# The down-projection of an MLP by one level of Strassen's scheme, on one Trainium2 core

## The chip, the cores and the metric

The kernel runs on one core of a Trainium2 chip. The core has TensorE (PE, with its weight loads shown as PEld), VectorE (DVE), ScalarE (ACT), GpSimd (POOL) and SyncE (SP), a memory SBUF of 128 partitions, accumulator banks (PSUM) that TensorE writes, and 16 DMA engines. The metric is the device time of one execution in microseconds (us), as the median of several runs.

## The reference

The program is one layer of a hybrid encoder for 1024 prompt tokens and 32 sample tokens, 1056 together. Three mixers (attention, a state space model, RWKV-7) write one merged activation; then

```python
x = layer_norm(ALPHA * x + merged @ prm['w_out'], prm['ln1_g'], prm['ln1_b'])
hidden = jnp.square(jax.nn.relu(x @ prm['w_up']))      # 1024 -> 4096
x = layer_norm(ALPHA * x + hidden @ prm['w_down'], prm['ln2_g'], prm['ln2_b'])   # 4096 -> 1024
```

Everything is float32. The change concerns the last two lines and the end of the first.

## The kernel before

**Products.** A float32 operand is split in a high part (a copy rounded by ScalarE) and a low part (what is left, subtracted by VectorE or GpSimd): `split3`. `mm3` then makes three matmuls per block: high x high, high x low, low x high. Its three lines (63, 65, 67) issue nearly all the matmuls here.

**Output projection and first normalisation** (in `tile_trunk`). Nine token tiles, 0 to 7 of 128 tokens and tile 8 of the 32 sample tokens, run in the order 0 to 8. `out_tile` multiplies, `out_ln` normalises on VectorE, and `out_turn` transposes the result on TensorE into `g.xr` (features on the partitions), stores it in HBM (`xr_d`) and, for the first half of the tokens, splits it into the operands B11 and B21. Tokens are halved at 528 (HT), which lies within tile 4. The turn of a tile is issued behind the product of the next.

**Up-projection** (`up_product`, `up_sums`, `x_operands`). It is already done by one level of Strassen's scheme (Winograd's form): per pair q of 128-wide hidden chunks (16 pairs) there are seven products instead of eight, with weight operands A11, A12, A22, S1 to S4 (VectorE makes the sums S, tile `ws`; `operand` splits them into `wo`, ScalarE and GpSimd) and token operands B11, B21, B22, T1 to T4 (tile `xo`, made once in `x_operands` from `xr` with the scratch tile `tr`). A product has 4 feature chunks x 2 blocks of 264 tokens x 3 matmuls = 24. The first two pairs run products 1 and 2 early, since these need only B11 and B21. Then each pair takes its products in the order ORD. Sums of products are taken on VectorE out of the banks (tiles `u`, `hx`; line 1629); ReLU and square follow on ScalarE, and `hx` (2112 columns) is stored in HBM as `h_d`.

**Down-projection** (the second half of `mlp`). It is a plain product. Eight rounds r load two pairs of hidden activations (`load_h`: `hr`, split by ScalarE and VectorE into `ho`) and four chunks of weights (`load_dn`, split by ScalarE and GpSimd), one round ahead. Within a round `down_part` runs 8 output tiles m with token blocks of 384, 384 and 288; after four chunks each block is added to `yacc` on VectorE (line 1742). `yacc` begins as the normalised x, times ALPHA (line 1740). The last round goes block by block (288, then three of 256), and `final_ln` normalises and stores the token tiles of a finished block, while the next block is multiplied. Behind the last block stand tiles 4 and 5.

**Order.** The Tile framework writes each engine's instruction stream beforehand by a simulated timeline: instructions of different steps may be interleaved, and each engine then runs its stream in that order.

Of the kernel before, what the change touches and what calls it, by code (L numbers as in the profile page):

```python
# [1496 lines left out]

def out_turn(g, i, pool, tag):

    nc = g.nc  # L1500
    s, n = tok_tiles()[i]
    z = g.z.pop(i)
    e = min(s + n, HT)
    for h in range(2):
        pt = pool.tile([P, 4, P], F32, tag=tag, name="pt")
        for k in range(4):
            c = (4 * h + k) * P
            nc.tensor.transpose(out=pt[:, k, :n], in_=z[:n, c:c + P], identity=g.ident[:n, :n])  # L1508
# [23 lines left out]
OSUM = (0, 2, 1, 0, 1, 0, 1, 0, 1)  # L1532
# [51 lines left out]

def up_sums(g, st, order):

    V = g.nc.vector
# [4 lines left out]
    sums = {"S1": (a21, w["A22"], ALU.add), "S2": ("S1", a11, ALU.subtract), "S3": (a11, a21, ALU.subtract), "S4": (a12, "S2", ALU.subtract)}

    def made(x):
        if isinstance(x, str):
            if x not in w:
                a, b, op = sums[x]
                a, b = made(a), made(b)
                w[x] = g.wb.tile([P, 512], F32, tag="ws", name="ws", bufs=NWS)
                V.tensor_tensor(out=w[x], in0=a, in1=b, op=op)  # L1600
            return w[x]
        return x

    ops = {}
    for n in order:
        x = PROD[n][0]
        ops[x] = operand(g, made(x))
    w.update(ops)


def up_product(g, st, n):
# [22 lines left out]
    def block(i):  # L1634
        return lambda c: st.hx[:, i, HC * c:HC * c + HC]

    if n == 1:
        for c in range(2):
            st.u[c] = g.wb.tile([P, HC], F32, tag="u", name="u", bufs=4)
            nc.scalar.activation(out=st.u[c], in_=st.bank[1, c], func=AF.Copy)  # L1640
    if n == 2:
        for c in range(2):
            nc.scalar.activation(out=block(0)(c), in_=st.bank[1, c], func=AF.Relu)
    new = st.made - {0}
    if 6 in st.made and "u2" not in st.made:
        add(u, 6, u)
        st.made.add("u2")
    if {"u2", 7} <= st.made and "u3" not in st.made:
        add(block(3), 7, u)
        st.made.add("u3")  # L1650
    if {"u3", 5} <= st.made and "c22" not in st.made:
        add(block(3), 5, block(3))
        st.made.add("c22")
    if n == 4:
        add(block(2), 7, u)
    if n == 3:
        add(block(1), 5, u)
    if len([i for i in st.made if isinstance(i, int)]) == 7:
        nc.scalar.activation(out=st.hx[:, 1:4], in_=st.hx[:, 1:4], func=AF.Relu)
        nc.scalar.activation(out=st.hx, in_=st.hx, func=AF.Square)  # L1660
        nc.sync.dma_start(out=g.h_d[st.q], in_=st.hx.rearrange("p b t -> p (b t)"))


NWS = 3
ORD0, ORD = (5, 7, 6, 4, 3), (1, 6, 7, 5, 2, 4, 3)
NP = 16


def x_operands(g):
# [4 lines left out]
    def new(pool, n):  # L1674
        return pool.tile([P, 2, 4, HT], F32R, tag="x", name="xo", bufs=n)

    for n in ("T1", "T3", "B22"):
        g.x[n] = new(g.xb, 3)
    r0, r1 = g.xr

    def cols(c, half):
        return slice(half * HT + HC * c, half * HT + HC * c + HC)

    def put(n, c, raw, eng):
        x = g.x[n][:, :, :, HC * c:HC * c + HC]
        split3(g, raw, x[:, 0], x[:, 1], eng)

    t = {}

    def sub(n, c, a, b):  # L1690
        t[n, c] = g.xb.tile([P, 4, HC], F32, tag="tr", name="tr", bufs=3)
        V.tensor_tensor(out=t[n, c], in0=a, in1=b, op=ALU.subtract)  # L1692

    for c in range(2):
        sub("T1", c, r0[:, :, cols(c, 1)], r0[:, :, cols(c, 0)])
        put("T1", c, t["T1", c], V)
        sub("T3", c, r1[:, :, cols(c, 1)], r0[:, :, cols(c, 1)])
        put("T3", c, t["T3", c], nc.gpsimd)
    g.x["T2"] = new(g.xa, 4)
    for c in range(2):  # L1700
        V.tensor_tensor(out=t["T1", c], in0=r1[:, :, cols(c, 1)], in1=t["T1", c], op=ALU.subtract)  # L1701
        put("T2", c, t["T1", c], V)
    for c in range(2):
        V.tensor_tensor(out=t["T1", c], in0=r1[:, :, cols(c, 0)], in1=t["T1", c], op=ALU.subtract)
        put("B22", c, r1[:, :, cols(c, 1)], nc.gpsimd)
    g.x["T4"] = new(g.xa, 4)
    for c in range(2):
        put("T4", c, t["T1", c], V)


def load_h(g, q):

    hr = g.wb.tile([P, 2 * T], F32, tag="hx", name="hr", bufs=2)
    g.nc.sync.dma_start(out=hr, in_=g.h_d[q])
    h = g.xa.tile([P, 2, 2 * T], F32R, tag="x", name="ho", bufs=4)
    split3(g, hr, h[:, 0], h[:, 1])
    return [(h[:, 0, T * j:T * j + T], h[:, 1, T * j:T * j + T]) for j in range(2)]


def load_dn(g, r):  # L1720

    raw = [load_raw(g, g.a["w_dn"][f // 2, f % 2]) for f in range(4 * r, 4 * r + 4)]
    return [[operand(g, x[:, 512 * h:512 * h + 512]) for x in raw] for h in range(2)]
# [349 lines left out]
```

## Time and profile before

| | us |
|---|---|
| median of 3 runs (1588.03 to 1594.25) | 1589.39 |
| the profiled execution | 1595.33 |
| its span, first to last instruction | 1593.6 |
| TensorE's mean granted clock | 0.957 of full |
| up-projection, from the end of the output projection at 826.7 | 358.7 |
| down-projection, to the last drain at 1577.9 | 392.5 |
| from there to the end | 15.7 |

A line of the page's groups reads: line, engine, operation, output<-inputs, shapes, count | busy us, mean ns of one | idle time of the engine just before, and what released it. A row of the table of stretches has the stretch, its length, then busy time and instruction count of each engine, the granted clock, the DMA share and GB/s. Matmuls are pipelined: the mean of a group (289 ns for 264 columns) is a latency, and the rate comes from counts in a stretch.

### The profile page before, as it was taken

To read this page: it belongs to the slowest core of one execution; us is meant where nothing else is said; L and a number is where in the kernel's file an instruction comes from. 1 tells how busy PE (TensorE), PEld (TensorE's weight loads), DVE (VectorE), ACT (ScalarE), POOL (GpSimd) and SP (SyncE) were. 2 spreads that over 40 slices of the span, in tenths; PEclk is the share of its full clock that TensorE was granted. 3 is DMA by queue.
4 is the path that set the end of the run, shared out by engine and by line. 5 is a ranking of instruction groups with operands and counts; after the bars stand their busy time and mean duration, and the time that the engine had idled before them with its cause. 6 is when DMAs were issued, how large, how long until landed. Compare 5 with 4: busy or idle time off the path is not lost.

```text
span 1593.6 us, 27633 instructions
## 1 busy us (share of the span) xinstructions
PE 1454.7 (91%) x11239; PEld 1301.5 (82%) x11239; DVE 824.1 (52%) x1528; ACT 580.7 (36%) x1043; POOL 553.1 (35%) x520
## 2 busy tenths in 40 slices
PE   7899989579999888899977999999998999999996
PEld 6889886466776656577857999999998999999995
DVE  8476959364655635446759433333323333332358
ACT  4344433315444554543324344444442221220112
POOL 3723563521111110212717444444441332322333
PEclk9999999889999999989997999999998999999998
DMA  5314471374332230235512222333364232212102
GB/s 185 126 66 177 145 192 36 83 160 99 87 97 71 65 75 21 73 111 165 157 44 78 100 100 103 108 108 108 109 265 168 108 108 107 86 49 81 53 27 84
DMA packets 127027, 166.83 MB, mean 105 GB/s; under 512 B 53136, under 2 KB 97860, under 8 KB 122168
## 3 DMA queue, kind: packets, MB, share of 16 engines
q1 hardware_dynamic: 106628, 141.46, 28.1%
q10 hardware_dynamic: 19920, 22.59, 4.3%
q8 instruction: 88, 1.44, 0.4%
q0 software_dynamic: 352, 1.01, 0.2%
q14 instruction: 39, 0.32, 0.1%
HBM read 110.67 MB, written 54.31 MB: 104 GB/s over the span
## 4 chain that ended last, share of the span: by engine, by line
PE 47%; DVE 5%; issue 1%; DMA 1%; POOL 1%; ACT 1%; DVEq 0%; SPq 0%; ACTq 0%; POOLq 0%
PE acc L63 15%; PE acc L67 15%; PE acc L65 15%; DVE ws L1600 1%; DVE o L1815 1%; DMA hr<-h_d 1%; DVE small L1374 0%; DVE z L1495 0%; PE pt L1508 0%; DVE tr L1692 0%; DVE yacc L1742 0%; DVE xo L50 0%; DVE tr L1701 0%; DMA wr<-in_w_up 0%; DVE ln L1374 0%
## 5 line engine op out<-in xcount | busy, mean ns | idle before, releaser
L50 POOL TENSOR_TENSOR wo<-wr,wo 128x512 fp32r<-128x512 f32 x112 | 176.3, 1577 | 319.9 <-ACT wo L49 319.9
L63 PE MATMUL acc<-xo,wo 128*128 128x264 f32 x896 | 258.5, 289 | 8.7 <-ACT u L1640 5.6
L65 PE MATMUL acc<-xo,wo 128*128 128x264 f32 x896 | 257.4, 287 | 0.0
L67 PE MATMUL acc<-xo,wo 128*128 128x264 f32 x896 | 256.8, 287 | 0.0
L49 ACT ACTIVATE wo<-wr 128x512 fp32r<-128x512 f32 x112 | 69.7, 629 | 342.0 <-PE acc L67 339.4
L63 PE MATMUL acc<-ho,wo 128*128 128x384 f32 (+2 forms) x800 | 183.8, 320 | 7.6 <-ACT ho L49 7.6
L65 PE MATMUL acc<-ho,wo 128*128 128x384 f32 (+2 forms) x800 | 182.8, 318 | 1.5 <-DVE ho L50 1.5
L67 PE MATMUL acc<-ho,wo 128*128 128x384 f32 (+2 forms) x800 | 182.2, 317 | 0.0
L1742 DVE TENSOR_TENSOR yacc<-yacc,acc 128x384 f32<-128x384 f32 (+2 forms) x176 | 80.1, 497 | 194.2 <-PE acc L67 194.0
L63 PEld LDWEIGHTS acc<-xo,wo 128*128 128x128 f32 x896 | 171.6, 192 | 9.4 <-ACT u L1640 6.0
L65 PEld LDWEIGHTS acc<-xo,wo 128*128 128x128 f32 x896 | 171.9, 192 | 0.0
L67 PEld LDWEIGHTS acc<-xo,wo 128*128 128x128 f32 x896 | 171.8, 192 | 0.0
L63 PEld LDWEIGHTS acc<-ho,wo 128*128 128x128 f32 x800 | 136.1, 190 | 7.9 <-ACT ho L49 7.9
L63 PE MATMUL acc<-xh,wmhi 128*128 128x384 f32 (+3 forms) x384 | 131.0, 342 | 8.2 <-ACT xh L49 7.1
L65 PEld LDWEIGHTS acc<-ho,wo 128*128 128x128 f32 x800 | 136.1, 189 | 1.9 <-DVE ho L50 1.8
L67 PEld LDWEIGHTS acc<-ho,wo 128*128 128x128 f32 x800 | 135.8, 188 | 0.0
L65 PE MATMUL acc<-xl,wmhi 128*128 128x384 f32 (+3 forms) x384 | 129.9, 338 | 2.7 <-DVE xl L50 2.6
L67 PE MATMUL acc<-xh,wmlo 128*128 128x384 f32 (+3 forms) x384 | 129.2, 336 | 0.0
L50 POOL TENSOR_TENSOR wo<-ws,wo 128x512 fp32r<-128x512 f32 x64 | 87.9, 1376 | 101.3 <-ACT wo L49 101.3
L1629 DVE TENSOR_TENSOR hx<-acc,u 128x264 f32<-128x264 f32 x96 | 41.6, 433 | 114.1 <-PE acc L67 112.6
L1257 PE MATMUL av<-ptk,vo 128*128 128x512 f32 (+5 forms) x204 | 75.8, 455 | 10.6 <-POOL ptk L1284 10.5
L63 PEld LDWEIGHTS acc<-xh,wmhi 128*128 128x128 f32 (+1 forms) x384 | 73.6, 192 | 11.8 <-ACT xh L49 7.4
(504 smaller groups left out, 2907.6 us busy)
## 6 DMA issues: line engine op xcount, KB each, us to landing
h_d<-hx SPq DMA_DIRECT2D x16, 1056.0 KB, 3.9
hr<-h_d SPq DMA_DIRECT2D x16, 1056.0 KB, 7.8
wr<-in_w_up SPq DMA_DIRECT2D x32, 512.0 KB, 3.5
wr<-in_w_dn SPq DMA_DIRECT2D x32, 512.0 KB, 3.5
ld<-rw SPq DMA_DIRECT2D x24, 320.0 KB, 5.8
wmraw<-in_w_m SPq DMA_DIRECT2D x12, 512.0 KB, 5.1
yacc<-xr_d ACTq DMA_DIRECT2D x2, 2112.0 KB
wo<-in_w_out SPq DMA_DIRECT2D x8, 512.0 KB, 3.7
```

The costliest lines, as they stand in the source:

```text
L49: nc.scalar.activation(out=hi, in_=ps, func=AF.Copy)
L50: (lo_eng or nc.vector).tensor_tensor(out=lo, in0=ps, in1=hi.bitcast(F32), op=ALU.subtract)
L63: nc.tensor.matmul(out=outs[i], lhsT=lh, rhs=rhs[i][0], start=start, stop=False, **kw)
L65: nc.tensor.matmul(out=outs[i], lhsT=lh, rhs=rhs[i][1], start=False, stop=False, **kw)
L67: nc.tensor.matmul(out=outs[i], lhsT=ll, rhs=rhs[i][0], start=False, stop=stop, **kw)
L1257: nc.tensor.matmul(out=po[:, c:n], lhsT=vo[:w, kt].rearrange("p a x -> p (a x)")[:, 64 * i:64 * i + P], rhs=pt[:w, c:n], start=kt == tiles ...
L1600: V.tensor_tensor(out=w[x], in0=a, in1=b, op=op)
L1629: V.tensor_tensor(out=to(c), in0=st.bank[key, c], in1=other(c), op=ALU.add)
L1742: nc.vector.tensor_tensor(out=y, in0=y, in1=ps[i][:, :n], op=ALU.add)
L1815: nc.vector.tensor_tensor(out=o[:n, c], in0=o[:n, c], in1=g.gb2[:n, 1, c], op=ALU.add)
```

## The change

**Token halves.** The 32 sample tokens are cut in two; each half of 528 begins with 16 of them, followed by four whole tiles (`pieces`). Blocks are 272 and 256 wide (CH). Tile 8 runs fourth, tile 7 last (OORD). Three pairs (NQ) have products 1 and 2 early: three of these six products are issued ahead of the last tile's turn and three behind it. Of the first half's tiles the operands B11, B21 are split as before; all low parts in `x_operands` go to VectorE. The scratch `z` of the last tile lies in a buffer of the weight ring.

**Store.** After ReLU and square `up_store` makes three token sums and one difference on VectorE (four instructions of 528 columns) and stores seven blocks instead of four: all the token operands of the second scheme.

**Down-projection.** Seven products in the order 1, 7, 5, 6, 4, 2, 3, each over all 16 pairs in 16 x 4 x 2 x 3 = 384 matmuls that accumulate in eight banks (4 output tiles x 2 blocks). Products 1 to 2 of the order run in 48 steps of two pairs. `Down.tokens` loads a step's token operand and splits it (ScalarE, VectorE); `Down.weights` loads 512 KB where it needs new weights, forms sums in the tile `c` on VectorE, and splits on ScalarE and VectorE. They are issued three steps ahead (AHEAD), the first two ahead of the last pair of the up-projection, in memory that this pair's products leave. After each product `down_drain` adds the banks to the four blocks of the output, and `down_after` combines blocks. Product 3 touches only one block; its split weights are kept, and it runs the 272-wide block, then the 256-wide one. The token tiles 0 to 3 are normalised in the first of these, 8 and 4 in the second, and 5, 6 and 7 behind it.

```diff
+OORD = (0, 1, 2, 8, 3, 4, 5, 6, 7)
-HC = HT // 2
+CH = ((0, 272), (272, 256))
+NP, NQ = 16, 3
+EARLY = ((0, 1), (1, 1), (0, 2), (1, 2), (2, 1), (2, 2))
...
+def up_store(g, st):
...
+    for out, a, b in ((ht[:, 0], hx[:, 0], h0), (hx[:, 0], hx[:, 2], hx[:, 0]), (ht[:, 1], hx[:, 2], ht[:, 0]), (ht[:, 2], hx[:, 1], ht[:, 1])):
+        V.tensor_tensor(out=out, in0=a, in1=b, op=ALU.subtract)
+    nc.sync.dma_start(out=g.h_d[st.q][:, 1:4], in_=hx)
+    nc.sync.dma_start(out=g.h_d[st.q][:, 4:7], in_=ht)
...
+DORD = (1, 7, 5, 6, 4, 2, 3)
+GQ = tuple((q, 2) for q in range(0, NP, 2))
+LASTQ = (((0, 3), (3, 3), (6, 3), (9, 3), (12, 2), (14, 2)), ((0, 4), (4, 4), (8, 4), (12, 4)))
+AHEAD = 3
...
+    def weights(self, n, q):
...
+        if n in (1, 2):
+            x = a
+            nc.sync.dma_start(out=x, in_=src(1, n))
+        elif n == 7:
+            x = tmp()
+            nc.sync.dma_start(out=c, in_=src(2, 1))
+            V.tensor_tensor(out=x, in0=a, in1=c, op=ALU.subtract)
+        elif n == 4 or n == 5:
+            x = tmp()
+            nc.sync.dma_start(out=x, in_=src(2, 2))
+            if n == 5:
+                V.tensor_tensor(out=c, in0=c, in1=x, op=ALU.add)
+                x = c
+        else:
+            V.tensor_tensor(out=c, in0=c, in1=a, op=ALU.subtract)
+            x = c
+        hi, lo = (ring(g, "wo", [P, 2, 512], F32R) for _ in range(2))
+        split3(g, x, hi, lo)
...
+def down_after(g, d, n):
...
+    elif n == 6:
+        V.tensor_tensor(out=y[2, 1], in0=y[2, 1], in1=y[1, 2], op=ALU.add)
+        V.tensor_tensor(out=y[2, 2], in0=y[2, 2], in1=y[1, 2], op=ALU.add)
+        V.tensor_tensor(out=y[1, 2], in0=y[1, 2], in1=d.r, op=ALU.add)
+        keep()
+        nc.scalar.dma_start(out=d.r, in_=g.xr_d[0][:, :, HT:T])
+        V.scalar_tensor_tensor(out=y[1, 2], in0=d.r, scalar=ALPHA, in1=y[1, 2], op0=ALU.mult, op1=ALU.add)
...
     nc = g.nc
-    sts = g.early + [Pair(q) for q in range(2, NP)]
+    sts = g.early + [Pair(q) for q in range(NQ, NP)]
+    for q, n in EARLY[:3]:
+        up_product(g, sts[q], n)
+    out_turn(g, OORD[-1], g.pacc, "acc")
...
+    for i, (n, (q0, m)) in enumerate(steps):
+        while made < min(len(steps), i + AHEAD + 1):
+            x = steps[made]
+            ops[x] = d.weights(x[0], x[1][0]), d.tokens(x[0], *x[1], (0, HT))
+            made += 1
...
+        if q0 == 0:
+            ps = [[g.pacc.tile([P, 512], F32, tag="acc", name="acc")[:, :w] for s, w in CH] for _ in range(4)]
+        ws, hs = ops.pop((n, (q0, m)))
+        for j in range(m):
+            for t in range(4):
+                wh, wl = (x[:, t * P:t * P + P] for x in ws[j])
+                mm3(nc, ps[t], wh, wl, [[x[:, s:s + w] for x in hs[j]] for s, w in CH], q0 + j == 0, q0 + j == NP - 1)
+        if q0 + m == NP:
+            for t in range(4):
+                for c in range(2):
+                    down_drain(g, d, n, t, c, ps[t][c])
+            down_after(g, d, n)
```

More of the change, by code (lines that the diff above doesn't have):

```diff
@@ L1634, in block, with done @@
     def block(i):
[L1635 to L1639, printed above, removed]
+        return lambda c: st.hx[:, i, CH[c][0]:CH[c][0] + CH[c][1]]
+    def done(x, *need):
+        return x not in st.made and set(need) <= st.made and not st.made.add(x)
+    for c, (s, m) in enumerate(CH):
+        if n == 1:
+            st.u[c] = g.wc.tile([P, CH[0][1]], F32, tag="u", name="u", bufs=6)[:, :m]
@@ L1640, in up_product @@
             nc.scalar.activation(out=st.u[c], in_=st.bank[1, c], func=AF.Copy)
+        if n == 2:
+            nc.scalar.activation(out=st.h0[:, s:s + m], in_=st.bank[1, c], func=AF.Relu)
     if n == 2:
[L1642 to L1645, printed above, removed]
+        nc.scalar.activation(out=st.h0, in_=st.h0, func=AF.Square)
+    if done("u2", 1, 6):
         add(u, 6, u)
-        st.made.add("u2")
@@ L1648, in up_product @@
[L1648 to L1653, printed above, removed]
+    if done("u3", "u2", 7):
+        add(block(2), 7, u)
+    if done("c22", "u3", 5):
+        add(block(2), 5, block(2))
     if n == 4:
-        add(block(2), 7, u)
+        add(block(1), 7, u)
     if n == 3:
[L1657 to L1661, printed above, removed]
@@ L1672, in x_operands @@
     V = nc.vector
[L1674 to L1692, printed above, removed]
@@ L1706, in x_operands @@
[L1706 to L1723, printed above, removed]
@@ L1745, with cut, sub, put @@
-LAST = ((768, 288), (0, 256), (256, 256), (512, 256))
-NR = 8
+    for i, n in enumerate(("T3", "T1", "B22")):
+        x_new(g, n, 4 + i)
+    (b11, b12), (b21, b22) = [[x[:, :, HT * j:HT * j + HT] for j in range(2)] for x in g.xr]
+    def cut(x, c):
+        s, m = CH[c]
+        return x[:, :, s:s + m]
+    def sub(out, a, b):
+        V.tensor_tensor(out=out, in0=a, in1=b, op=ALU.subtract)
+    def put(n, raw, c):
+        hi, lo = g.x[n]
+        split3(g, raw, cut(hi, c), cut(lo, c))
+    r = range(2)
@@ new lines, in x_operands @@
+    for c in r:
+        sub(cut(b11, c), cut(b12, c), cut(b11, c))
+        put("T1", cut(b11, c), c)
+    for c in r:
+        sub(cut(b12, c), cut(b22, c), cut(b12, c))
+        put("T3", cut(b12, c), c)
+    t = [g.wc.tile([P, 4, m], F32, tag="hx", name="xt", bufs=2) for s, m in CH]
+    for c in r:
+        sub(t[c], cut(b22, c), cut(b11, c))
+        put("B22", cut(b22, c), c)
+    x_new(g, "T2", 0)
+    for c in r:
+        put("T2", t[c], c)
+    for c in r:
+        sub(t[c], cut(b21, c), t[c])
```

349 lines of the change are left out of this document (232 added, 117 removed).

## The prediction

> **What bounds the kernel now.** I read the page first, then a table of stretches, then TensorE's waits in the two stretches that stood out.
>
> ```profile
> span 1593.6 us, 27633 instructions
> PE 1454.7 (91%) x11239; PEld 1301.5 (82%) x11239; DVE 824.1 (52%) x1528; ACT 580.7 (36%) x1043; POOL 553.1 (35%) x520
> PE 47%; DVE 5%; issue 1%; DMA 1%; POOL 1%; ACT 1%; DVEq 0%; SPq 0%; ACTq 0%; POOLq 0%
> ```
>
> TensorE (PE) is busy for 91% of the span, and it is the engine on which the chain of waits mostly runs. The change lies behind 826.7 us, where the last product of the output projection ends. So I cut the rest into stretches: the up-projection (826.7 to 1185.4), the down-projection (1185.4 to 1577.9), the tail, and the parts of each.
>
> ```profile
> core 0: us, PE busy (x) PEld busy (x) DVE busy (x) ACT busy (x) POOL busy (x), PEclk, DMA share, GB/s
> 826.70:1185.40 358.70, 336.74 (x2705) 335.79 (x2704) 154.48 (x247) 153.71 (x228) 171.30 (x120) 0.96 0.32 110
> 826.70:890.00 63.30, 41.34 (x278) 40.39 (x277) 53.60 (x47) 25.17 (x42) 38.20 (x19) 0.78 0.20 61
> 950.00:1150.00 200.00, 200.00 (x1646) 200.00 (x1645) 67.62 (x136) 86.82 (x128) 89.31 (x69) 1.00 0.30 103
> 1185.40:1577.90 392.50, 383.02 (x2472) 381.65 (x2470) 156.43 (x279) 78.80 (x109) 120.59 (x70) 0.99 0.26 94
> 1185.40:1207.00 21.60, 12.51 (x64) 11.74 (x63) 5.06 (x3) 5.98 (x4) 3.08 (x1) 0.80 0.83 326
> 1207.00:1530.00 323.00, 323.00 (x2014) 323.00 (x2013) 111.92 (x186) 60.24 (x70) 97.60 (x56) 1.00 0.24 84
> 1577.90:1593.60 15.70, 0.62 (x4) 0.20 (x2) 10.09 (x22) 2.31 (x8) 2.93 (x2) 0.58 0.29 116
> ```
>
> ```profile
> PE pt L1508 <- DVE z L1495: 13.2, 1, 13.2
> ...
> PE acc L63 <- ACT ho L49: 7.6, 1, 7.6
> ```
>
> Inside both stages TensorE never stops, at full clock. From these rows come two rates. Up: 200/1646 = 0.1215 us for a matmul of 264 columns, 0.460 ns a column. Down: 323/2014 = 0.1604 us for blocks of 384, 384 and 288 (mean 352), 0.456 ns a column. So short blocks cost nothing, and time goes by columns. The starts are another matter: 63.3 us with 41.3 busy at clock 0.78, after a wait of 13.2 for the last token tile's normalisation; and 21.6 us with 12.5 busy at 0.80, where the second hidden tile's load was late.
>
> **The work on TensorE.** Down before: 32 hidden chunks x 8 output tiles x 1056 tokens x 3 passes = 811,008 columns x 0.456 ns = 369.5 us. After: 7 products x 16 chunks x 4 tiles x 2 blocks x 3 = 2688 matmuls of 272 or 256 columns, 709,632 in all. I take the 264-column rate: 2688 x 0.1215 = 326.6. That is 42.9 less, on the path. Bounds: the two rates give 323.6 to 326.6. Up keeps its 2688 matmuls (blocks of 272 and 256 instead of two of 264): 326.6 before and after.
>
> **What each stage loses.** Seven token tiles are transposed within the down stage:
>
> ```profile
> 826.71 1.03 PE L1508 MATMUL pt<-ident,z 128*128 128x128 f32 x8
> ...
> 1535.18 2.46 PE L1795 MATMUL pt<-ident,yacc 128*128 128x128 f32 x21
> ...
> 814.70 1.28 DVE L1492 SCALAR_TENSOR_TENSOR z<-z,acc 128x512 f32<-128x512 f32 x2 [6.37 <-PE acc L67]
> ...
> 819.12 1.29 DVE L1495 SCALAR_TENSOR_TENSOR z<-z,ln,gb 128x1024 f32<-128x1024 f32 x1
> ```
>
> 56 transposes x 2.46/21 = 6.6. Down then loses 392.5 - 369.5 - 6.6 = 16.4. Up, with the transposes of two token tiles (1.0 each), loses 358.7 - 326.6 - 2.1 = 30.0.
>
> **Start of up.** Before, TensorE had nothing while the last tile was normalised, then four early products (24 matmuls, 2.9 us each), then it starved for operand sums. Now tile 7 is last instead of tile 8, and the early operands need only tiles 8 and 0 to 3. So three early products (8.7 us) stand behind the output projection and cover tile 7's normalisation, which takes 814.7 to 820.4 = 5.7 for such a tile. Three more (8.7) follow its transposes. What is late next are the operands T1, T3, B22, T2, T4.
>
> ```profile
> L1704 DVE TENSOR_TENSOR tr<-xr,tr 128x1056 f32<-128x1056 f32 x2 | 2.5, 1246 | 0.0
> ...
> L50 DVE TENSOR_TENSOR xo<-tr,xo 128x1056 fp32r<-128x1056 f32 x6 | 13.0, 2172 | 0.0
> ...
> L1600 DVE TENSOR_TENSOR ws<-wr 128x512 f32<-128x512 f32 x20 | 13.7, 687 | 1.4
> ```
>
> VectorE (DVE) now makes all of them: 8 subtractions and 10 low parts of 4 x 264 elements, 18 x 1.246 = 22.4 us, of which two subtractions can precede tile 7 (-2.5), plus four weight sums of 0.687 = 2.7: 22.6. The fourth product of the first pair, which needs T4, can come 8.7 + 3 x 2.9 = 17.4 us after tile 7 is transposed. So 5 us are late at the lone price; at the mean of the stretch before (2.172) the other 16 take 16 x 0.93 = 14.8 more, 20 late. GpSimd (POOL) had two of these splits then, and has none now. I take **10** of loss, nearer the lone price; bounds 0 and the old 30. The Trainium skill (SBUF — State Buffer, "Who interferes with whom") says the port pair that VectorE and GpSimd share is an exclusive lock; the two prices above agree, and by it alone the loss would be the 5.
>
> **Up, steady.** Each pair adds four subtractions of 528 elements (0.7 each by the 512 row) and stores 1.85 MB instead of 1.06. VectorE works 67.6 of 200 there and the DMAs 0.30 of their time, so both stay covered: 0. If the cover were gone, 14 pairs x 2.8 = 39.
>
> **The down steps.** 48 steps of two chunks each, 48 matmuls = 5.83 us, must be prepared three ahead.
>
> ```profile
> L50 DVE TENSOR_TENSOR ho<-hr,ho 128x2112 fp32r<-128x2112 f32 x16 | 39.2, 2452 | 14.5 <-ACT ho L49 14.5
> ...
> L1742 DVE TENSOR_TENSOR yacc<-yacc,acc 128x288 f32<-128x288 f32 x56 | 25.1, 449 | 8.5 <-PE acc L67 8.5
> L1742 DVE TENSOR_TENSOR yacc<-yacc,acc 128x256 f32<-128x256 f32 x24 | 9.7, 404 | 2.0 <-PE acc L67 1.7
> ...
> L49 ACT ACTIVATE wo<-wr 128x512 fp32r<-128x512 f32 x65 | 40.2, 629 | 264.9 <-PE acc L67 263.9 <-issue 1.0
> L49 ACT ACTIVATE ho<-hr 128x2112 fp32r<-128x2112 f32 x16 | 31.3, 1959 | 17.8 <-DMA hr<-h_d 17.8
> ...
> hr<-h_d SPq DMA_DIRECT2D x16, 1056.0 KB, 7.8
> ...
> wr<-in_w_dn SPq DMA_DIRECT2D x32, 512.0 KB, 3.5
> ...
> z<-in_xa SPq DMA_DIRECT2D x8, 512.0 KB, 7.0
> ```
>
> A step's two low parts (1024 and 1056 elements, half of 2452 each) and, in products 7, 5, 6, a weight sum (1.2) make 2.4 to 3.6 us of VectorE; ScalarE (ACT) has 1.0 + 1.3 = 2.3. Both fit under 5.83. Loads: 528 KB of tokens and, in 40 of the steps, 512 KB of weights, 1.06 MB in 5.83 us = 183 GB/s; the row 1185.4 to 1207 carried 326.
>
> **Product ends.** All eight accumulator banks belong to one product, so the next waits for its drains: 8 adds x 0.43 = 3.4 us of VectorE. The first pair of banks is full 18 matmuls (2.2 us) before the end, and each next tile's banks are wanted 0.73 later: covered if VectorE answers at once, up to 3.4 at each of six ends if not. Behind product 6 stand four operations of 2112 elements (4 x 2.45) and a 1056 KB load (7.8) in the queues of VectorE and ScalarE, 17.6 us against 17.5 of prepared steps. First operands: their memory is free before up ends, so the 16.4 at the start goes. I take **7** for the stage; bounds 0 and 6 x 3.4 + 17.6 = 38.
>
> **Tail.** Three token tiles (5, 6, 7) instead of two are normalised behind the last matmul, and the fourth scratch buffer makes tile 7 wait for tile 5's output.
>
> ```profile
> L1815 DVE TENSOR_TENSOR o<-o,gb 128x512 f32<-128x512 f32 x14 | 18.1, 1303 | 0.7 <-POOL o L1813 0.5
> L1374 DVE BATCH_NORM_STATS2 small<-pt 128x6 f32<-128x512 f32 x16 | 10.4, 683 | 0.2 <-PE pt L1795 0.2
> ...
> out_y<-o SPq DMA_DIRECT2D x8, 512.0 KB, 3.1
> ```
>
> One tile: 2 x (1.303 + 0.683) = 4.0, and 0.5 for two more drains: 15.7 becomes 20.2. Bounds: 0 and 4.0 + 3.1 + 0.5 = 7.6 added.
>
> **The sum.** Up: 1.0 + 326.6 + 1.0 + 10 = 338.6, that is -20.1. Down: 326.6 + 6.6 + 7 = 340.2, -52.3. Tail +4.5. Together -67.9. The profiled execution took 1595.33 (span 1593.6 and 1.7 around it), so the same execution would take 1527.4. It is 5.9 above the median of the runs, 1589.39, from which I forecast **1521.5**.
>
> **Rivals.**
> - *The starts stay unfilled.* The losses of 30.0 and 16.4 stay and only the columns count: -0.1 - 42.9 + 4.5 = -38.5, **1551**. For it: the long list of operands on one engine. Against: six early products in place of four, two of them ahead of the wait of 13.2.
> - *Product ends stall.* Loss 38 instead of 7: **1553**. For: VectorE's order is fixed beforehand, with splits between the drains. Against: it has 2 to 3 us free in each step.
> - *Loads pace the steps (slower).* If one queue's two loads land one after the other, a step takes p instead of 5.83, in 40 steps; the gain of 67.9 is gone at p = 7.53. 3.5 and half of 7.8 make 7.4, 1584; with the row of 7.0 it is 10.9, **1724**. Against: 326 GB/s with many loads in flight.
> - *The clock drops (slower).* Bank ends leave short pauses in every product, and the granted clock falls to 0.80 as in the row of 1185.4: 326.6/0.80 - 326.6 = +81.7, **1603**; from 0.83 on it is slower. Against: 1.00 over 323 us with banks turning over. The Trainium skill (TensorE: Matmul & The Clock Gate, "A second HAM failure mode: psum-queue depth-cycling") describes such a loss when accumulator banks are cycled with small pauses. By that rule this change would be slower; the trace so far does not bear it out, since the kernel before cycles eight banks at 1.00.
> - *Nothing is late:* all losses 0 and no longer tail: -89.4, **1500**.
>
> **Chances.** Forecast (1507 to 1538, its losses together off by up to 15) 0.62; starts 0.15; product ends 0.07; nothing late 0.06; loads 0.06, of which 0.02 near break-even; clock 0.04. 1504 to 1553 holds all but about 0.18 (loads, clock, the outer halves of the others). A measurement here can tell about 0.5%, 8 us: faster 0.90, same 0.02, slower 0.08.
>
> **What would show it.** Right: 2688 matmuls each up and down, 0.121 us apiece at clock 1.00, under 10 us of TensorE idle between 827 and 880, no wait at the change to down, waits at product ends below 1 us, a tail near 20. Wrong: TensorE waiting within products for the splits or for loads (loads), for drains at six places (ends), a clock under 0.9 (clock), or an idle first stretch (starts).

## The result

The changed kernel takes 1534.18 us (median of 4 runs, 1525.25 to 1539.79), the kernel before 1591.41 (1588.03 to 1594.25): a ratio of 0.9636, 95% interval 0.9582 to 0.969. The prediction was 1521.5, with 1504 to 1553 as its range: the time lies in the range and 12.7 above the forecast.

By the stages of the prediction, each read from the profiled execution (it took 1531.51, its span is 1529.3). Up runs from the end of the output projection to the last product of up, down from there to the start of the last drain (which adds the last bank to the output), the tail from there to the end:

| us | before | predicted | after |
|---|---|---|---|
| up | 358.7 | 338.6 | 344.4 |
| down | 392.5 | 340.2 | 343.2 |
| tail | 15.7 | 20.2 | 21.9 |
| sum | 766.9 | 699.0 | 709.5 |

In the changed kernel the last drain starts as the last product ends, at 1507.4. In the kernel before VectorE was busy with an output then, and the last drain started late:

```profile
1576.28 0.28 PE L67 MATMUL acc<-ho,wo 128*128 128x256 f32 x1
...
1576.60 1.43 DVE L1815 TENSOR_TENSOR o<-o,gb 128x512 f32<-128x512 f32 x1
1577.96 0.41 DVE L1742 TENSOR_TENSOR yacc<-yacc,acc 128x256 f32<-128x256 f32 x1
```

The last product ended at 1576.6 there, 1.3 us ahead of the table's boundary at 1577.9. Counted from the last product in both kernels, down was 391.2 us and the tail 17.0 before.

The sum fell by 57.4, which is the difference of the medians (57.2). The two spans differ by 64.3; the other 6.9 lie ahead of the change, where the code is the same: the output projection ended at 826.7 in the one execution and at 819.8 in the other.

### The profile page after: what moved, and what is told of

It reads as the page before. It is cut to its first block, busy times and chain, and to the rows that moved or that the text cites. A ratio compares the mean times of both kernels' runs of the same rounds, so it can differ in the third digit from the quotient of the medians.

```text
span 1529.3 us, 28349 instructions
## 1 busy us (share of the span) xinstructions
PE 1399.3 (92%) x11527; PEld 1245.0 (81%) x11527; DVE 953.1 (62%) x1586; ACT 637.3 (42%) x1123; POOL 436.7 (29%) x453
## 4 chain that ended last, share of the span: by engine, by line
PE 66%; DVE 15%; DMA 5%; ACT 5%; issue 4%; POOL 3%; SPq 0%; ACTq 0%; DVEq 0%; POOLq 0%
PE acc L65 17%; PE acc L63 16%; PE acc L67 16%; PE av L1257 2%; DVE y L761 2%; DVE tmp L760 1%; PE sc L63 1%; DMA h_d<-ht 1%; PE st L63 1%; DVE ws L1614 1%; DVE xo L50 1%; PE sc L65 1%; PE sc L67 1%; PE st L65 1%; PE st L67 1%
## 5 line engine op out<-in xcount | busy, mean ns | idle before, releaser
L63 PE MATMUL acc<-xo,wo 128*128 128x272 f32 (+1 forms) x896 | 256.3, 286 | 4.2 <-DVE u L1639 2.5
L65 PE MATMUL acc<-xo,wo 128*128 128x272 f32 (+1 forms) x896 | 254.9, 285 | 5.2 <-DVE xo L50 5.2
L67 PE MATMUL acc<-xo,wo 128*128 128x272 f32 (+1 forms) x896 | 255.4, 285 | 0.0
L67 PE MATMUL acc<-hop,wo 128*128 128x272 f32 (+1 forms) x896 | 197.0, 284 | 0.0
L65 PEld LDWEIGHTS acc<-xo,wo 128*128 128x128 f32 x896 | 169.7, 189 | 5.7 <-DVE xo L50 5.7
L63 PEld LDWEIGHTS acc<-xo,wo 128*128 128x128 f32 x896 | 169.5, 189 | 5.4 <-DVE u L1639 2.9
L67 PEld LDWEIGHTS acc<-xo,wo 128*128 128x128 f32 x896 | 169.9, 190 | 0.0
L63 PE MATMUL acc<-hop,wo 128*128 128x272 f32 (+1 forms) x768 | 161.5, 286 | 6.0 <-ACT hop L49 6.0
L65 PE MATMUL acc<-hop,wo 128*128 128x256 f32 (+1 forms) x768 | 161.7, 285 | 0.1
L67 PEld LDWEIGHTS acc<-hop,wo 128*128 128x128 f32 x896 | 144.3, 189 | 0.0
L63 PEld LDWEIGHTS acc<-hop,wo 128*128 128x128 f32 x768 | 119.9, 189 | 6.2 <-ACT hop L49 6.2
L2012 POOL TENSOR_TENSOR wr<-wr,gb 128x512 f32<-128x512 f32 (+1 forms) x16 | 22.0, 1401 | 355.6 <-ACT wr L2010 355.6
L65 PEld LDWEIGHTS acc<-hop,wo 128*128 128x128 f32 x768 | 121.0, 189 | 0.4 <-DVE hop L50 0.4
L50 POOL TENSOR_TENSOR wo<-ws,wo 128x512 fp32r<-128x512 f32 x64 | 91.9, 1438 | 93.4 <-ACT wo L49 93.4
L49 ACT ACTIVATE wo<-wr 128x512 fp32r<-128x512 f32 (+1 forms) x64 | 47.0, 738 | 134.5 <-PE acc L67 69.0
L50 POOL TENSOR_TENSOR wo<-wr,wo 128x512 fp32r<-128x512 f32 x48 | 66.9, 1395 | 98.7 <-ACT wo L49 96.1
L1639 DVE TENSOR_TENSOR hx<-acc,u 128x272 f32<-128x272 f32 x96 | 41.0, 429 | 73.6 <-PE acc L67 73.5
```

Of the source, the lines that this page charges most:

```text
L49: nc.scalar.activation(out=hi, in_=ps, func=AF.Copy)
L50: (lo_eng or nc.vector).tensor_tensor(out=lo, in0=ps, in1=hi.bitcast(F32), op=ALU.subtract)
L63: nc.tensor.matmul(out=outs[i], lhsT=lh, rhs=rhs[i][0], start=start, stop=False, **kw)
L65: nc.tensor.matmul(out=outs[i], lhsT=lh, rhs=rhs[i][1], start=False, stop=False, **kw)
L67: nc.tensor.matmul(out=outs[i], lhsT=ll, rhs=rhs[i][0], start=False, stop=stop, **kw)
L1639: V.tensor_tensor(out=to(c), in0=st.bank[key, c], in1=other(c), op=ALU.add)
```

## The profile after

From the page: its span, the engines, and the chain of work that ended last.

```profile
span 1529.3 us, 28349 instructions
PE 1399.3 (92%) x11527; PEld 1245.0 (81%) x11527; DVE 953.1 (62%) x1586; ACT 637.3 (42%) x1123; POOL 436.7 (29%) x453
PE 66%; DVE 15%; DMA 5%; ACT 5%; issue 4%; POOL 3%; SPq 0%; ACTq 0%; DVEq 0%; POOLq 0%
```

TensorE lost 55 us of work and is still the bound. The shares of this chain cannot be compared with those of the page before: there the chain could be followed back only to 705 us (its shares add up to 56%), here to the start of the span. Behind the output projection VectorE has 69 us of the chain before and 59 after, the DMAs 15 and 20. The new waits have to be looked for in the stretches. The table of stretches, with the three stages first, then the start of up, the steady up, the change to down (two rows) and the steady down:

```profile
819.82:1164.21 344.39, 332.84 (x2705) 330.70 (x2703) 212.98 (x312) 152.05 (x237) 153.73 (x109) 0.99 0.41 149
1164.21:1507.36 343.15, 335.03 (x2739) 334.22 (x2739) 222.82 (x260) 134.05 (x171) 14.96 (x12) 0.99 0.50 166
1507.36:1529.30 21.94, 3.72 (x25) 3.08 (x22) 14.57 (x32) 4.26 (x13) 7.09 (x6) 0.61 0.24 96
...
819.80:882.00 62.20, 51.30 (x387) 49.72 (x386) 53.92 (x60) 29.14 (x51) 33.47 (x19) 0.95 0.38 124
950.00:1150.00 200.00, 200.00 (x1652) 200.00 (x1652) 106.11 (x174) 87.84 (x136) 87.92 (x67) 1.00 0.37 136
1164.20:1170.20 6.00, 0.02 (x1) 0.00 (x0) 2.68 (x4) 5.07 (x4) 0.00 (x0) 0.77 1.08 410
1170.20:1180.00 9.80, 9.70 (x63) 9.39 (x64) 5.05 (x6) 3.02 (x3) 0.00 (x0) 0.79 1.00 405
1207.00:1450.00 243.00, 243.00 (x2000) 243.00 (x1999) 159.26 (x160) 96.70 (x113) 0.00 (x0) 1.00 0.48 151
```

In the steady stretches TensorE never stops, at clock 1.00: 243/2000 = 0.1215 us a matmul. The losses are at the two starts. At the start of up TensorE is idle for 10.9 of 62.2 us (22.0 of 63.3 before), while VectorE is busy for 53.9. At the change to down it does nothing for 6.0 us, and in the 9.8 us behind that, at clock 0.79, it runs 63 matmuls where 81 would fit; the DMAs are busy all through it. TensorE's waits from 819 us on say what came last each time (sum, times, longest):

```profile
PE acc L63 <- ACT hop L49: 6.0, 1, 6.0
PE pt L1994 <- ACT wr L2010: 5.6, 1, 5.6
PE acc L65 <- DVE xo L50: 5.2, 2, 3.6
PE acc L63 <- DVE u L1639: 2.5, 2, 2.1
PE pt L1514 <- DVE z L1495: 2.2, 1, 2.2
PE acc L63 <- DVE yacc L1845: 2.0, 2, 1.6
```

From the top: the first token operand of down (`hop`), the tail, the operands of up (`xo`, and `u`, the sums that stand in the same queue of VectorE), tile 7's normalisation, and the product ends of down, 2.0 us in all.

## The experiments

All runs were also timed, but the time of a whole run differs by up to 1% from one to the next: the output projection, the same code in all, ended between 819.8 and 832.3 us. The stages behind it repeat far better. Up took 344.3 to 344.6 us in six kernels with the same products there, the tail 21.7 to 22.0 in six; down took 343.2 to 344.2 in the five that leave it as it is, so a difference of 1 us in down says nothing. So the experiments are read by stages. The medians stand beside them, with their ratios to the kernel before as it was timed along with each (its medians were 1591.4 to 1595.8).

| us | up | down | tail | sum | median | ratio, interval |
|---|---|---|---|---|---|---|
| changed kernel | 344.4 | 343.2 | 21.9 | 709.5 | 1534.2 | 0.9636, 0.9582 to 0.969 |
| e6_plain | 343.2 | 379.4 | 17.6 | 740.2 | 1564.7 | 0.9801, 0.9764 to 0.9838 |
| e1_late | 344.4 | 338.9 | 23.1 | 706.3 | 1527.8 | 0.9565, 0.9534 to 0.9597 |
| e1c_act | 344.3 | 342.9 | 21.9 | 709.1 | 1539.3 | 0.962, 0.9572 to 0.9669 |
| e1e_weights | 344.6 | 338.9 | 23.1 | 706.6 | 1532.8 | 0.9611, 0.9573 to 0.9649 |
| e1d_late_ends | 344.5 | 334.8 | 23.1 | 702.4 | 1530.5 | 0.9606, 0.9569 to 0.9643 |
| e7_nopool | 339.8 | 343.3 | 21.8 | 704.8 | 1531.5 | 0.9603, 0.9561 to 0.9645 |
| e5_pool | 347.3 | 344.2 | 21.7 | 713.2 | 1541.1 | 0.9662, 0.9623 to 0.9701 |
| e2b_unsplit | 344.7 | 343.8 | 22.0 | 710.5 | 1536.4 | 0.9641, 0.9601 to 0.968 |
| e2_turn | 346.3 | 344.0 | 21.9 | 712.3 | 1543.3 | 0.967, 0.9625 to 0.9715 |
| e3_tail | 344.4 | 345.0 | 17.8 | 707.2 | 1530.5 | 0.9586, 0.9554 to 0.9618 |
| e8_all | 340.7 | 335.7 | 17.8 | 694.2 | 1521.9 | 0.9543, 0.9511 to 0.9574 |

### How much of the gain is the scheme: e6_plain

The changed kernel with the plain down-projection of the kernel before, and without the token sums and their stores in up.

```diff
-        if q + 1 == NP:
-            d = Down(g)
...
+    hs, ws = {0: [d.load_h(q) for q in range(2)]}, {0: d.load_dn(0)}
+    d.load_y()
+    for r in range(NR):
+        if r + 1 < NR:
+            hs[r + 1], ws[r + 1] = [d.load_h(q) for q in (2 * r + 2, 2 * r + 3)], d.load_dn(r + 1)
+            h = [x for p in hs.pop(r) for x in p]
+            for m in range(KD):
+                d.part(m, BLK, d.pairs(ws[r], h, m), r == 0)
```

> The token halves, the six early products and the up-projection of the changed kernel, with the down-projection of the kernel before: eight rounds over all 4096 hidden values in blocks of 384, 384 and 288 (last round 272, 256, 272, 256), and neither the token sums nor their stores behind each pair. Nothing is left out. By my sum the scheme itself is worth 42.9 us of columns in the steady stage (811,008 to 709,632 at 0.456 to 0.460 ns) and the new start of up is worth the rest: this kernel should lie 43 to 55 us above the changed one, at 1575 to 1590, with a first stretch of up as after (10 to 17 us lost) and a down stage of about 385 to 395. Rival: the up stage's gain comes with the scheme and not with the halves (it would then be as before, 358.7): then it lies at the time of the kernel before, 1589, or above. Rival: the columns do not set the down stage: then it lies within 30 us of the changed one.

The time is below the range that I gave, 1564.7. Its stages in the table of stretches:

```profile
820.19:1163.41 343.22, 334.38 (x2706) 332.95 (x2705) 149.25 (x250) 154.45 (x242) 161.38 (x116) 0.98 0.35 120
1163.41:1542.83 379.42, 377.53 (x2458) 377.16 (x2458) 151.01 (x276) 78.68 (x111) 120.14 (x70) 1.00 0.27 98
1542.83:1560.40 17.57, 1.75 (x17) 1.51 (x14) 11.01 (x22) 3.70 (x10) 4.97 (x4) 0.68 0.30 120
```

Against the kernel before, up is 15.5 us shorter, down 11.8 (plain too, its first operands no longer late), and the tail 0.6 longer, both counted from the last product: -26.7 without the scheme. From here to the changed kernel it is +1.2, -36.3 and +4.4: -30.7 with it (the two ratios, 0.9801 and 0.9636, make it 26, give or take 10). So not quite half of the gain came from the new halves, the early products and the freed memory together; how it is shared among these was not tried. The first row also prices what the scheme adds to up, the token sums and their larger stores: 1.2 us.

The scheme was to save 42.9 us of columns in down and saved 36.3 there. Where is the rest?

### The change to down: e1_late, e1c_act, e1e_weights, e1d_late_ends

Two readings of the 6.0 us were open: the tokens land late, or ScalarE, which splits them, takes them late. The rows of ScalarE in the changed kernel (start, us, and what ended the idle time before) fit both, since a weight split, ReLU and square all stand ahead of the first split of tokens:

```profile
1165.08 1.06 ACT L49 ACTIVATE wo<-wd 128x1024 fp32r<-128x1024 f32 x1 [3.40 <-DMA h_d<-ht]
1166.05 1.51 ACT L1677 ACTIVATE hx<-hx 128x1584 f32<-128x1584 f32 x1
1167.58 1.52 ACT L1678 ACTIVATE hx<-hx 128x1584 f32<-128x1584 f32 x1
1169.10 1.08 ACT L49 ACTIVATE hop<-hraw 128x1056 fp32r<-128x1056 f32 x1
```

e1_late moves transfers: the weight loads of steps three to eight behind their tokens, and the y loads.

```diff
-            ops[x] = d.weights(x[0], x[1][0]), d.tokens(x[0], *x[1], (0, HT))
+            h = d.tokens(x[0], *x[1], (0, HT))
+            with g.tc.issue_after(last_traced(g, mybir.EngineType.SP)) if made < 8 else nullcontext():
+                ops[x] = d.weights(x[0], x[1][0]), h
             made += 1
+            if made == 5:
+                with g.tc.issue_after(last_traced(g, mybir.EngineType.Activation)):
+                    d.load_y()
```

> The changed kernel lost 6.0 us at the change from up to down (TensorE waits for the first split tokens), and a clock of 0.79 to 0.87 behind it. Here the weight loads of the third to eighth down step stand on SP's queue behind the token loads of their own step, and the loads of the output's start values (y) on ScalarE's queue behind the fifth step's split; so ScalarE's splits of those weights move back too. Nothing is left out. Theory A (the transfers: 4 MB of weights and 3 MB of y values are issued in one burst ahead of or beside the tokens, at 353 to 412 GB/s): the tokens land earlier, the wait falls from 6.0 to 0 to 1 us, the stage from 343 to 334 to 337 us, the time by 6 to 10 us. Theory B (ScalarE's fixed order: the first token split stands behind the fourth weight split and the last pair's ReLU and square): only what the moved weight split took goes, the wait stays at 3 us or more (ReLU and square of the last pair, at 1166 to 1169, are still ahead or close), 0 to 3 us in all. Rival C: later weights are late themselves and TensorE waits in steps 3 to 8: slower by up to 10 us.

e1c_act leaves the transfers and moves ScalarE's work.

```diff
+    with g.tc.issue_after(g.hop) if g.hop else nullcontext():
+        nc.scalar.activation(out=hx, in_=hx, func=AF.Relu)
+        nc.scalar.activation(out=hx, in_=hx, func=AF.Square)
...
+            h = d.tokens(x[0], *x[1], (0, HT))
+            with g.tc.issue_after(last_traced(g, mybir.EngineType.Activation)) if made < 8 else nullcontext():
+                ops[x] = d.weights(x[0], x[1][0]), h
```

> All loads are issued as in the changed kernel; only ScalarE's order differs: the first token split stands ahead of the last pair's ReLU and square, and the weight splits of the third to eighth step behind their token splits. Nothing is left out. Theory A (transfers): the first tokens land no earlier, ScalarE waits for them itself, the wait of TensorE at the change stays at 4 to 7 us, and the time is the same within 3 us or, as the last pair's ReLU and square are then behind that wait, longer by 2 to 6. Theory B (ScalarE's order): the wait falls from 6.0 to 0 to 2 us and the time by 4 to 8.

In e1c_act nothing is gained (sum 709.1 for 709.5). With nothing ahead of it ScalarE waits for the tokens itself. The timelines of SP (issue of loads) and ScalarE:

```profile
1156.68 3.27 SPq L1802 DMA_DIRECT2D wd<-in_w_dn  x5
1160.06 0.44 SPq L1684 DMA_DIRECT2D h_d<-hx  x1
1160.55 1.47 SPq L1802 DMA_DIRECT2D wd<-in_w_dn  x2
...
1162.91 0.50 SPq L1802 DMA_DIRECT2D wd<-in_w_dn  x1
1163.60 7.20 SPq L1784 DMA_DIRECT2D hraw<-h_d  x4
```

```profile
1179.24 1.08 ACT L49 ACTIVATE hop<-hraw 128x1056 fp32r<-128x1056 f32 x1 [7.65 <-DMA hraw<-h_d]
```

Eight weight loads of 512 KB go out ahead of the first 528 KB of tokens, which are issued at 1163.6 and used at 1179.2, 15.6 us later. The kernel e1d_late_ends, below, has two weight loads ahead (SP, then ScalarE):

```profile
1162.77 2.06 SPq L1786 DMA_DIRECT2D hraw<-h_d  x3
```

```profile
1168.26 1.08 ACT L49 ACTIVATE hop<-hraw 128x1056 fp32r<-128x1056 f32 x1 [0.65 <-DMA hraw<-h_d]
```

There it is 5.5 us. In e1_late the wait at the change is gone, but down falls by only 4.3 us, since a new wait came, the first of these (TensorE's waits in e1_late; its lines lie 3 further on behind line 1774):

```profile
PE acc L63 <- ACT yacc L1851: 2.2, 1, 2.2
...
PE acc L63 <- DVE yacc L1848: 2.0, 2, 1.6
```

At the first product's end ScalarE, which copies all eight banks while VectorE adds them, had splits of later steps ahead of the copies. The granted clock fell behind this wait, and TensorE ran 51 matmuls in 10 us, the wait included, where 82 would fit:

```profile
1214.00:1224.00 10.00, 7.79 (x51) 7.58 (x50) 10.00 (x15) 4.38 (x10) 0.00 (x0) 0.83 0.28 76
```

e1e_weights asks which of the two kinds of load mattered: it has e1_late's order of the weights, with the y loads where they were.

> As the run with late loads, but only the weight loads of the third to eighth down step are behind their tokens; the 3 MB of y loads are issued where the changed kernel has them, on ScalarE's queue at 1160 and 1165. Nothing is left out. Theory A (the 4 MB of weights ahead of the tokens in one queue are what delays them): the wait at the change is 0 to 1 us as with both moved. Theory B (y shares the transfer engines as much): 2 to 4 us of the 6.0 stay. With both the down stage was 338.9.

Down is 338.9, as with both: the weights alone did it. The other run, e1d_late_ends, is e1_late with the split of the eleventh step behind the first copies.

```diff
-        while made < min(len(steps), i + AHEAD + 1):
+        while made < min(len(steps), i + AHEAD + 1) and i != 7:
             x = steps[made]
+            with g.tc.issue_after(last_traced(g, mybir.EngineType.Activation)) if i == 8 else nullcontext():
...
```

> As the run with late weight loads, which took away the wait of 6.0 at the change to down but got a new wait of 2.2 at the first product's end, where ScalarE had two splits of the next product ahead of its copies of the accumulator banks. Here the split of the eleventh step stands behind these copies. Nothing is left out. Theory A: the 2.2 go and nothing comes in their place, so the down stage is 336 to 337 us (338.9 in that run, 343.2 in the changed kernel). Theory B: the bank turnover there was late for another engine (VectorE's eight adds, which also stand behind weight sums): 1 to 2 us of wait stay, now for VectorE, and the stage stays at 338 to 339.

Theory A, and a little more: 334.8 us. Against e1_late that is 4.1 less: the wait of 2.2 and, at a clock of 0.83 over 10 us, some 1.7 behind it. In the table of stretches, the stage and then the first 6 us of it:

```profile
1174.38:1509.20 334.82, 332.79 (x2738) 332.30 (x2738) 220.71 (x259) 132.06 (x169) 14.89 (x12) 1.00 0.52 169
1174.40:1180.40 6.00, 6.00 (x51) 6.00 (x51) 4.50 (x6) 5.99 (x6) 0.00 (x0) 1.00 1.05 399
```

The DMAs carry as much as in the changed kernel (399 GB/s), but TensorE now runs from the first microsecond. The same burst costs 8.3 us or nothing, by the order in which its parts go out: 6.0 of waiting, and some 2 of low clock behind it.

One thing stays open. In the three runs with late weights the tail is 1.2 us longer; the arithmetic ends at the same distance from the last product, so it lies in the last store. e8_all has the same order and does not show it.

### The start of up: e7_nopool, e5_pool

At 1.2 us an operation the prediction had found 5 us of loss here, at 2.2 us 20. In the changed kernel's timeline of VectorE both prices stand (1.21 at 848.6, where GpSimd was idle from 847.0 to 849.8), and GpSimd is at work in 33.5 of the 62.2 us (the row of 819.80 above): 19 low parts of weights. VectorE in the changed kernel:

```profile
837.37 2.32 DVE L1715 TENSOR_TENSOR xr<-xr 128x1024 f32<-128x1024 f32 x1
839.79 2.14 DVE L1715 TENSOR_TENSOR xt<-xr 128x1024 f32<-128x1024 f32 x1
841.86 1.77 DVE L1614 TENSOR_TENSOR ws<-wr,ws 128x512 f32<-128x512 f32 x1
843.55 2.31 DVE L50 TENSOR_TENSOR xo<-xr,xo 128x1024 fp32r<-128x1024 f32 x1
```

e7_nopool gives those weights' low parts to VectorE, e5_pool gives the low parts of two token operands back to GpSimd.

```diff
-    w.update({x: operand(g, made(x)) for x in [PROD[n][0] for n in order]})
+    w.update({x: operand(g, made(x), V if st.q < 3 else None) for x in [PROD[n][0] for n in order]})
```

> The low parts of the weights of the first three pairs are made on VectorE, not on GpSimd, so GpSimd does nothing in the start of up. VectorE gets some 13 operations of 0.68 us, 8.8 us more. Nothing is left out. In the changed kernel the subtractions and low parts between 837 and 868 took 2.1 to 2.3 us where GpSimd worked beside them and 1.2 where it did not, 11.5 us in all above the lone price, and VectorE never stopped. Theory A (the price is contention with GpSimd): they take 1.2 to 1.3, VectorE's stretch is 1 to 4 us shorter, and the up stage is 0 to 4 us shorter than 343.6. Theory B (the price belongs to these shapes): they stay at 2.1 to 2.3, and the up stage is 5 to 9 us longer.

```diff
-        split3(g, raw, cut(hi, c), cut(lo, c))
+        split3(g, raw, cut(hi, c), cut(lo, c), nc.gpsimd if n in ("T3", "B22") else None)
```

> The low parts of T3 and B22 (four operations of about 1024 elements) are made on GpSimd again, as before the change. Nothing is left out. In the changed kernel VectorE is busy without a stop from 835 to 870 at the start of up; these four take 1.2 to 2.4 us each there, 8 us. Theory A (any work on GpSimd slows VectorE's operations beside it, and GpSimd needs longer for the same): the up stage is the same or up to 6 us longer than the 344.4 of the changed kernel. Theory B (VectorE's list is simply too long): 4 to 8 us shorter.

In e7_nopool the same four operations, with GpSimd still:

```profile
842.92 1.22 DVE L1715 TENSOR_TENSOR xr<-xr 128x1024 f32<-128x1024 f32 x1
...
845.27 1.21 DVE L1715 TENSOR_TENSOR xt<-xr 128x1024 f32<-128x1024 f32 x1
846.40 0.68 DVE L1614 TENSOR_TENSOR ws<-wr,ws 128x512 f32<-128x512 f32 x1
847.00 1.21 DVE L50 TENSOR_TENSOR xo<-xr,xo 128x1024 fp32r<-128x1024 f32 x1
```

They take about half the time. The start of up in this run, to be read against the row of 819.80 above:

```profile
825.30:887.50 62.20, 55.42 (x425) 54.21 (x424) 53.12 (x80) 30.20 (x53) 6.92 (x5) 0.95 0.45 150
```

VectorE does more and is done sooner: up falls by 4.6 us, a little more than the 0 to 4 of theory A. In e5_pool it grows by 2.9, as theory A has it. Here two engines on one list of work were slower than one.

### The cover by early products: e2b_unsplit, e2_turn

The prediction let three early products cover tile 7's normalisation. In the changed kernel only two did; the weights of the third were split only from 828.8 on, and it then stood between tile 7's transposes:

```profile
828.83 0.33 PE L1514 MATMUL pt<-ident,z 128*128 128x128 f32 x1 [2.18 <-DVE z L1495]
...
833.46 0.93 PE L1514 MATMUL pt<-ident,z 128*128 128x128 f32 x7
```

```diff
-    for q, n in EARLY[:3]:
+    for q, n in EARLY[:2]:
         up_product(g, sts[q], n)
     out_turn(g, OORD[-1], g.pacc, "acc")
+    with g.tc.issue_after(last_traced(g, mybir.EngineType.PE)):
+        up_product(g, sts[EARLY[2][0]], EARLY[2][1])
```

> In the changed kernel only two of the three early products ran ahead of the last tile's turn; the third stood between its first and its other seven transposes (828.8 and 833.5), since its weights were split only when tile 7's normalisation had ended; VectorE idled from 830.0 to 835.3. Here all eight transposes stand ahead of the third product. Nothing is left out. Theory A (the turn's second part is what is late): tile 7 is there 4.6 us earlier, VectorE's chain of operands, which then bounds the start, begins at 831 instead of 835, and the up stage, 343.6 us from the first early product to the last product, becomes 339 to 341. Theory B (the weight sums in VectorE's order wait for their loads, which landed at 832 to 835, whatever tile 7 does): 343 to 344. Theory C (TensorE's own work bounds it): 343 to 345, as a transposed tile sooner only moves the same work.

Theory A falls: up is 344.7 for 344.4 (343.9 for 343.6 from the first early product), as theories B and C had it. The tile is transposed earlier and copied no earlier, as ScalarE has two weight splits ahead of the copies, and their load lands late; VectorE in turn waits for the copies. ScalarE, then VectorE in e2b_unsplit:

```profile
841.19 1.15 ACT L49 ACTIVATE wo<-wr 128x512 fp32r<-128x512 f32 x2 [2.66 <-DMA wr<-in_w_up]
842.25 1.06 ACT L1517 ACTIVATE xr<-pt 128x512 f32<-128x512 f32 x2
```

```profile
842.86 1.41 DVE L1715 TENSOR_TENSOR xr<-xr 128x1024 f32<-128x1024 f32 x1 [4.36 <-ACT xr L1517]
```

In the changed kernel VectorE waits for such a load itself, 5.3 us from 830.0 to 835.3, ahead of its long list (its group from 835 to 869):

```profile
L1614 DVE TENSOR_TENSOR ws<-wr 128x512 f32<-128x512 f32 x6 | 5.4, 910 | 5.3 <-DMA wr<-in_w_up 5.3
```

In the changed kernel, in e2b_unsplit and in e7_nopool alike, SyncE issues the first of these weight loads within 0.1 us of the end of tile 7's normalisation, whose scratch `z` has one of the buffers of their ring. No run moved them, so it is open what holds them and what earlier loads would be worth.

e2_turn takes the cover away: tile 7's turn stands ahead of the loop over `EARLY[:3]`.

> The cover is undone: tile 7's turn stands ahead of all six early products, so TensorE has nothing from the last product of the output projection (819.8 in the changed kernel) to the turn (828.8). Nothing is left out. My prediction counted three products of 2.9 us as work that fills this wait. Theory A (what fills the wait is gained): two products, 5.8 us, ran there, so the up stage is 5 to 7 us longer than in the run with the eight transposes together, from 345 to 350. Theory B (VectorE's chain of operands bounds the start, and the early products only fill another hole behind, where TensorE idled 11.5 us between 845 and 870): within 1.5 us of that run.

Up is 346.3: the 5.8 us of cover are worth 1.9 against the changed kernel, 1.6 against e2b_unsplit: just outside the 1.5 of theory B, far from the 5 to 7 of theory A. TensorE stood still for 8.0 us ahead of the turn there, for 2.2 before, but behind the turn its waits were 5.2 us instead of 8.7. Cover ahead of a wait is worth little when the same work would fill a hole behind it.

### The tail, and all together: e3_tail, e8_all

```diff
-    finals = {0: {1: (0,), 2: (1,), 3: (2,), 4: (3,)}, 1: {1: (8,), 2: (4,), 3: (5,)}}
+    finals = {0: {1: (0,), 2: (1,), 3: (2,), 4: (3,)}, 1: {0: (8,), 1: (4,), 2: (5,)}}
```

> One of the three token tiles that are normalised behind the last matmul (tile 5) moves ahead of it, beside the last tiles' products; nothing is left out. The tail of the changed kernel, from the last product's end to the end, is 21.9 us. If it is a chain of VectorE work of about 4.0 us a tile plus the wait of tile 7 for tile 5's output (0.7), it becomes 17 to 18, less than the span of the changed kernel by 4 to 5 us. Rival: a chain of latencies of the last tile alone (transposes, statistics, normalisation, store) sets it: 20 to 22 as before. Second rival: the tile's transposes wait for its drains within the products, and TensorE waits there: the tail is shorter by 4, and the stretch before it longer by as much.

The tail is 17.8 us, 4.1 less, so a tile behind the last matmul costs 4.1. Down is 1.9 longer: 1.1 of it is the wait at the change (7.1 for 6.0; it was 5.8 to 6.8 in the other kernels with the same loads), the other 0.8 about what the tile's eight transposes take, which moved into the stage (0.9 at the prediction's 2.46/21). e8_all joins the three edits that each shortened a stage: e1d_late_ends, e7_nopool and e3_tail.

> Three edits that each shortened one stage, together: late weight and y loads with the split behind the first banks' copies (down 334.8 for 343.2), low parts of the first three pairs' weights on VectorE (up 339.7 for 344.4 from the end of the output projection), tile 5 normalised ahead of the last matmul (tail 17.8 for 21.9). Nothing is left out. Theory A (the three stages are independent, and the earlier ends do not meet a new wait): up 340, down 335 to 336, tail 18 to 19, which is 15 to 17 us less than the changed kernel behind the end of the output projection; 1515 to 1520. Theory B (with up shorter, the seam's transfers are late again, or the tail's drains push into the products): half of it, 7 to 10 us.

```profile
820.26:1160.96 340.70, 332.87 (x2707) 331.02 (x2706) 209.79 (x329) 154.34 (x239) 124.80 (x94) 0.99 0.43 152
1160.96:1496.68 335.72, 333.69 (x2746) 333.20 (x2746) 224.82 (x268) 133.54 (x174) 16.32 (x13) 1.00 0.52 170
1496.68:1514.50 17.82, 1.82 (x17) 1.50 (x14) 11.28 (x23) 2.77 (x9) 5.15 (x4) 0.63 0.24 97
```

Theory A in the main: 15.2 us less than the changed kernel behind the output projection (694.2 for 709.5), a median of 1521.9 over 6 runs, and a ratio of 0.9543 (0.9511 to 0.9574) to the kernel before, just clear of the changed kernel's interval. The median lies just above the 1515 to 1520 that I gave, the tail just below its 18.

## Why the prediction was right, and where it was off

**Columns: right.** 2688 matmuls at 0.1215 us, clock 1.00, in the steady stretches of up and of down. The larger part of the gain comes from there: 36.3 us in down between e6_plain and the changed kernel.

**Start of up: mis-sized, 15.7 lost where I took 10** (344.4 - 326.6 - 2.1; the 1.2 of the added store are part of it). 10.9 of it are idle time at the start, some 3 a clock of 0.95 over these 62.2 us. The bounds were right, and so were the two prices of an operation, 1.2 and 2.2; the choice between them failed. I took the lone price because GpSimd no longer had any of these operands, and forgot the weights that it splits in the same stretch. e7_nopool shows that with GpSimd still the price is 1.2, and up 4.6 shorter. Even so it loses 11.1, where the lone price gave 5: it has 14 weight splits more on VectorE (9.5 us), and my list left out VectorE's wait of 5.3 us for weight loads. The Trainium skill (SBUF — State Buffer, "Who interferes with whom") has the rule that a VectorE operation with two inputs in SBUF contends with GpSimd's reads; 2.3 against 1.2 us agrees with it, but the 5 us that I drew from it left out GpSimd's work on the weights. The cover by early products, the other part of this step, was counted at three products over 5.7 us of normalisation. Two products ran, the normalisation took 9.0 (819.8 to 828.8), as three low parts of early operands (3.7 us) stand within it on VectorE, and the cover was worth 1.9 us.

**Added store: right.** Taken as 0, measured as 1.2 (e6_plain) out of a bound of 39.

**First operands of down: the step that failed.** "First operands: their memory is free before up ends, so the 16.4 at the start goes." The memory was free, and e6_plain, which uses it, has no wait. But I had checked the loads only in the steady state, 183 GB/s, and not at the change, where the weights of eight steps (4 MB) go out at once, with the y loads beside them. There the DMAs are full at 405 to 410 GB/s, and weights that are needed later went out ahead of tokens that are needed first. That cost 8.3 us (e1d_late_ends). As a rival I had loads that pace the steps; they never do, TensorE is busy for 243 of 243 us.

**Product ends: too dear.** 7 taken, 2.0 measured; and six token tiles, not seven, are transposed within down (5.6 for 6.6). So it is luck that down as a whole came out only 3.0 above the forecast: the 8.3 at its start were not in the sum, and 6.0 elsewhere were too much. The clock stays at 1.00 while all eight banks turn over, with waits of 1.6 us at most; in e1_late, with a wait of 2.2, it did fall, to 0.83 over 10 us. The rule in TensorE: Matmul & The Clock Gate of the Trainium skill ("A second HAM failure mode: psum-queue depth-cycling"), by which I had the clock as a rival, does not show in the changed kernel.

**Tail: right, but for the boundary.** In the table it is +6.2 for +4.5. But the 15.7 from which I started begins at a drain that was 1.3 us late; from the last product the tail grew from 17.0 to 21.9, by 4.9. A tile costs 4.1 as I had it (4.0, e3_tail), and the wait for the fourth buffer that I named is there, 0.7 us. e6_plain, with two tiles, has a tail 0.6 longer than before; what sets that was not tried.

Up +5.8, down +3.0, tail +1.7 make the 10.5 by which the sum is off (from the last product, down +4.3 and tail +0.4). Of the other 2.2, 2.0 are in the base: with a fourth run the median of the kernel before is 1591.41, 2.0 higher than the one I started from.

Of the signs that I had named for a right forecast, the matmul's 0.121 us at clock 1.00 held. TensorE idled 10.9 us at the start of up for under 10, waited 6.0 at the change for none, and 1.6 at one product end for below 1.

## What to carry to other kernels

Where a stage begins, add up all loads that are issued around its first matmul, not only those of a steady step, and send them in the order of first use: the same bytes at the same rate cost 8.3 us or none. When you price an operation of VectorE, list what GpSimd does in that stretch, weights included, before you choose between two prices; giving GpSimd's part to VectorE can be the faster way. And a change that comes with a new order of work should be run with its core taken out: here 26.7 of 57.4 us did not need the scheme.

## What the hardware showed beyond that

- Subtractions of 1024 elements with both inputs in SBUF took 1.21 us on VectorE with GpSimd still and as much as 2.3 beside it, those of 512 elements 0.68 and as much as 1.77.
- After 6.0 us without work TensorE's granted clock was 0.79 in the next 9.8 us, a loss of some 2 us on top of the wait. A wait of 2.2 us at a product end went with a clock of 0.83 over the 10 us around it (e1_late); behind one of 1.6 us the clock stayed at 1.00 (the changed kernel, 10 us from 1454.3).
- With all DMA engines busy, loads and stores together moved 399 to 410 GB/s, and 528 KB took 15.6 us to be usable behind eight loads of 512 KB, 5.5 behind two.
- Up took the same within 0.3 us in six kernels, one execution of each, and down within 1.0 us in five, while the end of the part ahead of them, the same code, differed by 12.5.
